# A two-layer hybrid trunk on one core: how the first weights of a new phase are prepared

## Chip, cores, metric

The kernel runs on one core of one Trainium2 chip. The metric is the device time of one execution in microseconds, as the median of several runs. The five engines are named as in the profile: PE (TensorE matmul, PEld its weight load), DVE (VectorE), ACT (ScalarE), POOL (GpSimd) and SP (SyncE, which issues the DMAs here).

## What is computed

256 tokens of width 2048 go through two layers, all in float32. Layer 0 mixes tokens with a Conformer convolution, layer 1 with differential attention; each is followed by a squared-ReLU MLP with 8192 hidden channels:

```python
for i in range(DEPTH):                                # DEPTH = 2
    mod = cond @ ada_w[i] + ada_b[i]                  # cond = silu(c)
    sh_m, sc_m, g_m, sh_f, sc_f, g_f = split(mod, 6)
    h = x * (1.0 + sc_m) + sh_m
    y = conformer_conv(h, ...) if i == 0 else diff_attention(h, ...)
    x = layer_norm(ALPHA * x + g_m * y, ln_mix_g[i], ln_mix_b[i])
    h = x * (1.0 + sc_f) + sh_f
    y = squared_relu_mlp(h, mlp_w1[i], ...)           # square(relu(h @ w1 + b1)) @ w2 + b2
    x = layer_norm(ALPHA * x + g_f * y, ln_ffn_g[i], ln_ffn_b[i])
```

## The kernel before

Every large product is made of three. A float32 operand is split into `hi`, a cast to the matmul's `fp32r` type on ACT, and `lo = x - hi` on DVE or POOL; PE then adds hi by hi (line 578), hi by the weights' lo (580) and lo by the weights' hi (581). Activations stand transposed in two buffers of 16 chunks of 128 channels each (`hm_hi` and `hm_lo` in the MLPs, `ha_hi` and `ha_lo` in the attention). Weights come in pieces of 1 MB, 128x2048, each handled as two **halves** of 128x1024: a half is one cast `wh_...`, one subtraction `wl_...` and, for two chunks and both token tiles, 12 matmuls of 128x512.

`run_jobs` walks a list of jobs, two halves each as a rule. `fetch(n)` prepares halves up to number n, four ahead of PE; their buffers rotate through four slots (`wsp`), so a half can be cast only when PE is through with the half four places earlier. ACT's order is left to the scheduler; PE's is as written, DVE's as written from the second convolution product on.

At three places the trunk goes from one weight matrix to one that needs the finished x of this one: convolution to first MLP (near 488 us of the trace), first MLP to attention (near 1232), attention to second MLP (near 1642). These are the **changes**. The last job before each (`tail`) has four halves; it does token tile 0 whole, then tile 1. So while PE works on tile 1, tile 0 is finished: `w2g`/`wo_g`/`pw_g` (line 727) multiplies by the gate, line 728 adds to `z`, then come statistics, `rs` (1/sqrt by a power on POOL, line 120), `nb` (653) and the normalising of four quarters of `z`, two on ACT (660), two on DVE (662). `feat_t` transposes the tile in four blocks on PE (`hm_t`, `ha_t`, 453), applies 1+scale and shift (`hm_h`, `ha_h`: blocks 0 and 2 on ACT, 458, blocks 1 and 3 on DVE, 461) and splits it (411 and 414; the lo of block 3 on POOL). The scale and shift columns come from `h_scalars` (740 to 743), which `prep` calls. The first job after a change (`lead`) has four halves as well and needs blocks 0 and 1 of a tile.

In `lead` jobs the subtractions of halves 1, 2 and 3 are POOL's (`POOL_LEAD`), in `tail` jobs those of halves 1 and 3. `base_x` multiplies `z` by the norm's gain (and in the attention adds its bias) on POOL, a quarter of the columns at a time (line 697, 699); `defer(first + step * q, ...)` sets after how many ticks. A tick is one half of an ordinary job.

## Time and profile before

| | |
|---|---|
| median of 3 runs | 2395.34 us (2389.94 to 2396.66) |
| the profiled execution | 2392.99 us, its span 2390.9 us |
| PE busy | 2279.8 us (95%) |
| PEld | 1816.8 us (76%) |
| DVE | 1763.9 us (74%) |
| ACT | 1095.2 us (46%) |
| POOL | 204.6 us (9%) |
| mean granted PE clock | 0.985 |

Times in the trace count from the start of the span; the 2.1 us by which the execution is longer lie around it. Busy shares are means over stages that differ, so PE at 95% leaves open where the other 5% lie.

### The profile page before, as it was taken

Reading aid. Unit: us, or ns where it says so; the run is one execution under the profiler, and the core shown is the slowest. Engines: PE = TensorE matmul, PEld = TensorE weight load, DVE = VectorE, ACT = ScalarE, POOL = GpSimd, SP = SyncE. Lnnn points to the kernel's source line nnn. Section 1 sums busy time; section 2 is a strip of 40 time slices with the busy share of each in tenths; the row PEclk is TensorE's granted clock in tenths of the full one; section 3 lists DMA queues with packets and bytes.
Section 4 is the critical chain, followed back from the end, with each engine's and each line's share of the span. In section 5 each row is a group of like instructions: output and inputs, shape, how many; then the busy total and the mean of one; then the engine's idle time right before and its main releaser. Section 6 shows DMA issues by size and latency. Waiting matters only on the chain.

```text
span 2390.9 us, 28653 instructions
## 1 busy us (share of the span) xinstructions
PE 2279.8 (95%) x11169; PEld 1816.8 (76%) x11169; DVE 1763.9 (74%) x2010; ACT 1095.2 (46%) x1498; POOL 204.6 (9%) x138
## 2 busy tenths in 40 slices
PE   5899998999999999999989999998999999999997
PEld 4576646778788888888867888876888888888885
DVE  5787787978787888878869776886875565555666
ACT  3333674255435445445444554544443443443442
POOL 0000001131200000000034001013111000000002
...
GB/s 346 331 321 305 134 250 384 347 187 331 319 323 289 313 316 280 318 315 284 301 182 240 228 181 235 235 315 134 297 257 204 183 194 194 181 189 194 193 219 98
DMA packets 270955, 606.47 MB, mean 254 GB/s; under 512 B 10974, under 2 KB 44388, under 8 KB 257508
## 3 DMA queue, kind: packets, MB, share of 16 engines
...
q14 instruction: 48, 0.39, 0.0%
...
## 4 chain that ended last, share of the span: by engine, by line
PE 79%; DVE 10%; DMA 4%; ACT 2%; issue 2%; SPq 1%; POOL 0%; DVEq 0%; ACTq 0%; POOLq 0%
PE w_ps L578 18%; PE w_ps L581 18%; PE w_ps L580 18%; DMA w_w<-in_mlp_w_dram 2%; DVE aacc L249 2%; PE pw_ps L503 2%; PE cv L784 2%; PE pw_ps L504 2%; PE pw_ps L505 2%; PE aps L290 1%; PE qkv_q_ps L581 1%; PE qkv_v_ps L581 1%; PE qkv_v_ps L578 1%; PE qkv_v_ps L580 1%; PE qkv_q_ps L580 1%
## 5 line engine op out<-in xcount | busy, mean ns | idle before, releaser
L543 DVE TENSOR_TENSOR wl_w<-w_w,wh_w 128x1024 fp32r<-128x1024 f32 x502 | 621.6, 1255 | 347.0 <-ACT wh_w L542 346.7
L542 ACT CAST wh_w<-w_w 128x1024 fp32r<-128x1024 f32 x512 | 539.2, 1056 | 736.6 <-PE w_ps L581 569.3
L578 PE MATMUL w_ps<-wh_w,hm_hi 128*128 128x512 f32 x1024 | 403.0, 394 | 4.5 <-ACT hm_hi L411 4.5
L580 PE MATMUL w_ps<-wl_w,hm_hi 128*128 128x512 f32 x1024 | 400.1, 391 | 2.4 <-DVE wl_w L543 2.4
L578 PE MATMUL w_ps<-wh_w,u_hi 128*128 128x512 f32 x1024 | 401.2, 392 | 0.0
L581 PE MATMUL w_ps<-wh_w,hm_lo 128*128 128x512 f32 x1024 | 400.1, 391 | 0.9 <-DVE hm_lo L414 0.9
L580 PE MATMUL w_ps<-wl_w,u_hi 128*128 128x512 f32 x1024 | 399.9, 391 | 0.0
L581 PE MATMUL w_ps<-wh_w,u_lo 128*128 128x512 f32 x1024 | 399.7, 390 | 0.0
L316 DVE SCALAR_TENSOR_TENSOR acc<-adaw,cond,acc 128x2048 f32<-128x2048 f32 (+1 forms) x105 | 243.9, 2323 | 0.1
L578 PEld LDWEIGHTS w_ps<-wh_w,hm_hi 128*128 128x128 f32 x1024 | 192.9, 188 | 48.5 <-ACT hm_hi L411 6.2
L580 PEld LDWEIGHTS w_ps<-wl_w,hm_hi 128*128 128x128 f32 x1024 | 192.9, 188 | 43.2 <-DVE wl_w L543 4.1
L581 PEld LDWEIGHTS w_ps<-wh_w,hm_lo 128*128 128x128 f32 x1024 | 192.7, 188 | 42.8 <-DVE hm_lo L414 2.7
L578 PEld LDWEIGHTS w_ps<-wh_w,u_hi 128*128 128x128 f32 x1024 | 192.9, 188 | 42.3 <-issue 1.7
L581 PEld LDWEIGHTS w_ps<-wh_w,u_lo 128*128 128x128 f32 x1024 | 193.0, 189 | 40.2
L580 PEld LDWEIGHTS w_ps<-wl_w,u_hi 128*128 128x128 f32 x1024 | 193.0, 188 | 40.0 <-DVE wl_w L543 0.2
L543 POOL TENSOR_TENSOR wl_w<-w_w,wh_w 128x1024 fp32r<-128x1024 f32 x10 | 24.0, 2405 | 1118.2 <-ACT wh_w L542 1118.2
L503 PE MATMUL pw_ps<-wh_pw,h_hi 128*128 128x512 f32 x256 | 107.0, 418 | 9.7 <-ACT wh_pw L491 4.1
L504 PE MATMUL pw_ps<-wl_pw,h_hi 128*128 128x512 f32 x256 | 102.7, 401 | 3.6 <-DVE wl_pw L492 3.6
L505 PE MATMUL pw_ps<-wh_pw,h_lo 128*128 128x512 f32 x256 | 102.3, 400 | 0.0
L492 DVE TENSOR_TENSOR wl_pw<-w_pw,wh_pw 128x1024 fp32r<-128x1024 f32 x64 | 77.8, 1222 | 26.2 <-ACT wh_pw L491 26.0
L491 ACT CAST wh_pw<-w_pw 128x1024 fp32r<-128x1024 f32 x64 | 66.0, 1052 | 48.6 <-PE pw_ps L505 40.8
L503 PEld LDWEIGHTS pw_ps<-wh_pw,h_hi 128*128 128x128 f32 x256 | 49.6, 194 | 39.0 <-issue 15.2
...
## 6 DMA issues: line engine op xcount, KB each, us to landing
w_w<-in_mlp_w_dram SPq DMA_DIRECT2D x256, 1024.0 KB, 5.6
...
```

The lines of the kernel that those rows point to most:

```text
L249: nc.vector.scalar_tensor_tensor(st["acc"], wv[:, kc % per, :], cond[:, kc:kc + 1], st["acc"], ALU.mult, ALU.add)
L316: nc.vector.scalar_tensor_tensor(st["acc"], w, cond[:, kc:kc + 1], st["acc"], ALU.mult, ALU.add)
L491: nc.scalar.copy(hq, rq)
L492: nc.vector.tensor_tensor(lq, rq, hq.bitcast(F32), op=ALU.subtract)
L503: nc.tensor.matmul(pss[t], lhsT=xh, rhs=wh, start=(kc == first), stop=False)
L504: nc.tensor.matmul(pss[t], lhsT=xh, rhs=wl, start=False, stop=False)
L505: nc.tensor.matmul(pss[t], lhsT=xl, rhs=wh, start=False, stop=(kc == last))
L542: nc.scalar.copy(hi, rq)
L543: eng.tensor_tensor(lo, rq, hi.bitcast(F32), op=ALU.subtract)
L578: nc.tensor.matmul(pss[tt], lhsT=xh, rhs=wh, start=(kc == 0 and job["bias"] is None), stop=False)
L580: nc.tensor.matmul(pss[tt], lhsT=xh, rhs=wl, start=False, stop=False)
L581: nc.tensor.matmul(pss[tt], lhsT=xl, rhs=wh, start=False, stop=(kc == nk - 1))
```

## The change

- The first halves of a `lead` job get buffers of their own: one half in the first MLP, two in the attention and the second MLP (`lead` is now that number). Half 0 lives in two buffers of the rotation `X`, half 1 in two new buffers of the pool `late`. They no longer wait for a slot, and `fetch` is called for them while PE is still at tile 0 of the `tail` job.
- `POOL_LEAD` is empty: all subtractions of `lead` halves are DVE's.
- In the attention and the second MLP `prep` (`h_scalars`) is called when the `tail` job begins.
- ACT runs in written order from the beginning of a `tail` job before a change to the end of the `lead` job, and only there.
- The fourth half's subtraction is written behind the blocks' steps (`low`), lo parts of the blocks are flushed earlier.
- `base_x` starts at 18 ticks in place of 6.

```diff
-POOL_LEAD = (1,2,3)
+POOL_LEAD = ()
...
+                    home = (None, "x", "late")[2 * i + q + 1] if lead and 2 * i + q < lead else None
+                    halves.append((f"{key}_{i}", srcs[i], q, pump, nc.gpsimd if pool else nc.vector, home))
...
+    def fetch(n, low=None):
...
-            hi = wsp.tile([P, 1024], F32R, tag="whi", name=f"wh_{name}_{q}")
-            lo = wsp.tile([P, 1024], F32R, tag="wlo", name=f"wl_{name}_{q}")
+            if home == "x":
+                hi = work.tile([P, 1024], F32R, tag="X", name=f"wh_{name}_{q}", bufs=3)
+                lo = work.tile([P, 1024], F32R, tag="X", name=f"wl_{name}_{q}", bufs=3)
+            elif home == "late":
+                hi = late["pool"].tile([P, 1024], F32R, tag="whi", name=f"wh_{name}_{q}")
+                lo = late["pool"].tile([P, 1024], F32R, tag="wlo", name=f"wl_{name}_{q}")
...
             nc.scalar.copy(hi, rq)
-            eng.tensor_tensor(lo, rq, hi.bitcast(F32), op=ALU.subtract)
+            if low is None:
+                eng.tensor_tensor(lo, rq, hi.bitcast(F32), op=ALU.subtract)
+            else:
+                low.append(lambda lo=lo, rq=rq, hi=hi, eng=eng: eng.tensor_tensor(
+                    lo, rq, hi.bitcast(F32), op=ALU.subtract))
...
+                nxt = jobs[n + 1] if n + 1 < len(jobs) else None
+                own, more = job["own"], nxt["own"] if nxt is not None else 0
+                if more:
+                    change = tc.manual_schedule(engines={mybir.EngineType.Activation})
+                    change.__enter__()
                 fetch(h + 4)
                 tail = []
+                if more and nxt["prep"] is not None and nxt["prep"][0]:
+                    nxt.pop("prep")[1]()
+                    nxt["prep"] = None
...
-                        if t == NT - 1:
-                            fetch(h + j + AHEAD)
+                        if t == NT - 1 and not more and not own:
+                            fetch(h + 4 + j)
+                        if t == NT - 1 and more and j >= 2:
+                            fetch(h + 4 + min(more + j - 1, 3))
                         steps = half(j, [t])
+                        if t == 0 and more and 1 <= j <= more:
+                            fetch(h + 4 + j)
+                        if t == NT - 1 and own:
+                            fetch(h + 4 + max(j + 1, own))
...
+                            low = []
                             if feat:
                                 feat.pop(0)()
+                                fetch(h + 4 + 4, low)
                             tail = steps[0]() or []
                             while tail or feat:
                                 if tail:
                                     tail.pop(0)()
+                                flush()
                                 if feat:
                                     feat.pop(0)()
+                                if low and not tail:
+                                    low.pop(0)()
...
+                if own:
+                    change.__exit__(None, None, None)
...
-            base_x(ln_g, None, f"basem{i}", 6, 4)
+            base_x(ln_g, None, f"basem{i}", 18, 4)
...
-                add_group(f"w1_{i}_{q}_{g}", lambda: cur["hT"], wtiles(mlp_w1[i], 0, KC, n0), pump=pump, lead=first,
+                add_group(f"w1_{i}_{q}_{g}", lambda: cur["hT"], wtiles(mlp_w1[i], 0, KC, n0), pump=pump, lead=(i + 1) * first,
...
-        base_x(ln_ffn_g[0], ln_ffn_b[0], "basea", 6, 5)
+        base_x(ln_ffn_g[0], ln_ffn_b[0], "basea", 18, 5)
```

How the instructions stand now is shown for the change into the attention; the change into the second MLP reads alike. PE's order is the same before and after throughout the program. VectorE first, at the end of the first MLP's tail job: `w2g_3_3_0` is the gating of tile 0, `wl_qkv_q_0_0` the first half of the attention's weights. Before:

```order
L727 TENSOR_TENSOR w2g_3_3_0_9481<-w_0_3_3_ps_9383,gbm_4883 128x512
L728 TENSOR_TENSOR z<-z,w2g_3_3_0_9481 128x512
L1276 BN_STATS mlp_st_3111<-z 128x6
L642 BN_AGGR lna_mv<-mlp_st_3111 128x2
L647 TENSOR_SCALAR lna_rs<-lna_mv 128x1
L543 TENSOR_TENSOR wl_qkv_q_0_0_9499<-w_qkv_q_0_9496,wh_qkv_q_0_0_9498 128x1024
L653 SCALAR_TENSOR_TENSOR lna_nb<-lna_mv,lna_rs 128x1
L662 TENSOR_SCALAR z<-z,lna_mv,lna_rs 128x512 x2
L740 TENSOR_SCALAR ha_s_9526<-mod_1_5845 128x16
L741 SCALAR_TENSOR_TENSOR ha_mul<-cols_ln,ha_s_9526 128x16
L742 TENSOR_TENSOR ha_add<-cols_ln,ha_s_9526 128x16
L743 TENSOR_TENSOR ha_add<-ha_add,mod_0_6880 128x16
```

After, where `ha_s` to `ha_add` are the scale and shift columns:

```order
L772 TENSOR_SCALAR ha_s_9464<-mod_1_5848 128x16
L773 SCALAR_TENSOR_TENSOR ha_mul<-cols_ln,ha_s_9464 128x16
L774 TENSOR_TENSOR ha_add<-cols_ln,ha_s_9464 128x16
L775 TENSOR_TENSOR ha_add<-ha_add,mod_0_6883 128x16
L552 TENSOR_TENSOR wl_qkv_q_0_0_9484<-w_qkv_q_0_9481,wh_qkv_q_0_0_9483 128x1024
L552 TENSOR_TENSOR wl_qkv_q_0_1_9494<-w_qkv_q_0_9481,wh_qkv_q_0_1_9493 128x1024
L759 TENSOR_TENSOR w2g_3_3_0_9503<-w_0_3_3_ps_9386,gbm_4886 128x512
L760 TENSOR_TENSOR z<-z,w2g_3_3_0_9503 128x512
L1308 BN_STATS mlp_st_3111<-z 128x6
L674 BN_AGGR lna_mv<-mlp_st_3111 128x2
L679 TENSOR_SCALAR lna_rs<-lna_mv 128x1
L685 SCALAR_TENSOR_TENSOR lna_nb<-lna_mv,lna_rs 128x1
```

The columns and two weight halves have moved ahead of tile 0's gating, where before they stood behind its normalising (the columns) or on POOL (half 1).

VectorE a little later, from tile 1's `rs` on, with the blocks 1, 0, 1 of tile 0. Before:

```order
L647 TENSOR_SCALAR lna_rs<-lna_mv 128x1
L461 TENSOR_SCALAR ha_h_9568<-ha_t_9567,ha_mul,ha_add 128x128 x4
L414 TENSOR_TENSOR ha_lo<-ha_h_9548,ha_hi 128x4x128
L653 SCALAR_TENSOR_TENSOR lna_nb<-lna_mv,lna_rs 128x1
L662 TENSOR_SCALAR z<-z,lna_mv,lna_rs 128x512 x2
L414 TENSOR_TENSOR ha_lo<-ha_h_9568,ha_hi 128x4x128
L461 TENSOR_SCALAR ha_h_9598<-ha_t_9597,ha_mul,ha_add 128x128 x4
L414 TENSOR_TENSOR ha_lo<-ha_h_9586,ha_hi 128x4x128
```

After, where `wl_qkv_q_1_1` is half 3 and the two `ha_h` rows in succession are block 3 of tile 0 and block 1 of tile 1:

```order
L679 TENSOR_SCALAR lna_rs<-lna_mv 128x1
L414 TENSOR_TENSOR ha_lo<-ha_h_9553,ha_hi 128x4x128
L461 TENSOR_SCALAR ha_h_9577<-ha_t_9576,ha_mul,ha_add 128x128 x4
L685 SCALAR_TENSOR_TENSOR lna_nb<-lna_mv,lna_rs 128x1
L694 TENSOR_SCALAR z<-z,lna_mv,lna_rs 128x512 x2
L414 TENSOR_TENSOR ha_lo<-ha_h_9577,ha_hi 128x4x128
L554 TENSOR_TENSOR wl_qkv_q_1_1_9564<-w_qkv_q_1_9530,wh_qkv_q_1_1_9563 128x1024
L414 TENSOR_TENSOR ha_lo<-ha_h_9595,ha_hi 128x4x128
L461 TENSOR_SCALAR ha_h_9608<-ha_t_9607,ha_mul,ha_add 128x128 x4
L461 TENSOR_SCALAR ha_h_9657<-ha_t_9656,ha_mul,ha_add 128x128 x4
```

The lo of block 0 now stands ahead of block 1's `ha_h`; half 3 has come in, and block 3 of tile 0 stands behind the lo of block 2.

ScalarE over the same stretch, from the first cast of the attention's weights on. Before:

```order
L542 CAST wh_qkv_q_0_0_9498<-w_qkv_q_0_9496 128x1024
L542 CAST wh_qkv_q_0_1_9514<-w_qkv_q_0_9496 128x1024
L542 CAST wh_qkv_q_1_0_9533<-w_qkv_q_1_9531 128x1024
L660 ACTIVATE z<-z,lna_nb,lna_rs 128x512 x2
L542 CAST wh_qkv_q_1_1_9612<-w_qkv_q_1_9531 128x1024
L458 ACTIVATE ha_h_9548<-ha_t_9547,ha_add,ha_mul 128x128 x4
L411 CAST ha_hi<-ha_h_9548 128x4x128
L411 CAST ha_hi<-ha_h_9568 128x4x128
L458 ACTIVATE ha_h_9586<-ha_t_9585,ha_add,ha_mul 128x128 x4
L411 CAST ha_hi<-ha_h_9586 128x4x128
L660 ACTIVATE z<-z,lna_nb,lna_rs 128x512 x2
L411 CAST ha_hi<-ha_h_9598 128x4x128
```

After:

```order
L550 CAST wh_qkv_q_0_0_9483<-w_qkv_q_0_9481 128x1024
L550 CAST wh_qkv_q_0_1_9493<-w_qkv_q_0_9481 128x1024
L692 ACTIVATE z<-z,lna_nb,lna_rs 128x512 x2
L550 CAST wh_qkv_q_1_0_9532<-w_qkv_q_1_9530 128x1024
L458 ACTIVATE ha_h_9553<-ha_t_9552,ha_add,ha_mul 128x128 x4
L411 CAST ha_hi<-ha_h_9553 128x4x128
L550 CAST wh_qkv_q_1_1_9563<-w_qkv_q_1_9530 128x1024
L411 CAST ha_hi<-ha_h_9577 128x4x128
L692 ACTIVATE z<-z,lna_nb,lna_rs 128x512 x2
L458 ACTIVATE ha_h_9595<-ha_t_9594,ha_add,ha_mul 128x128 x4
L411 CAST ha_hi<-ha_h_9595 128x4x128
L411 CAST ha_hi<-ha_h_9608 128x4x128
```

The casts of halves 2 and 3 have moved behind tile 0's normalising and behind block 0's split.

## Rows read from the trace of the kernel before

**Rows 1.** Timeline, TensorE, attention change: start us, us, instruction, count [idle before <-releaser].

```profile
1231.83 0.39 PE L581 MATMUL w_ps<-wh_w,u_lo 128*128 128x512 f32 x1
1234.27 1.97 PE L453 MATMUL ha_t<-ident,z 128*128 128x128 f32 x16 [2.06 <-ACT z L660]
1242.68 0.80 PE L578 MATMUL qkv_q_ps<-wh_qkv_q,ha_hi 128*128 128x512 f32 x1 [6.44 <-ACT ha_hi L411]
...
1245.37 0.79 PE L581 MATMUL qkv_q_ps<-wh_qkv_q,ha_lo 128*128 128x512 f32 x1 [1.47 <-DVE ha_lo L414]
1245.96 0.63 PE L578 MATMUL qkv_q_ps<-wh_qkv_q,ha_hi 128*128 128x512 f32 x1
1246.39 0.63 PE L580 MATMUL qkv_q_ps<-wl_qkv_q,ha_hi 128*128 128x512 f32 x1
...
1255.28 0.50 PE L578 MATMUL qkv_q_ps<-wh_qkv_q,ha_hi 128*128 128x512 f32 x1 [0.94 <-ACT ha_hi L411]
...
1262.38 0.50 PE L580 MATMUL qkv_q_ps<-wl_qkv_q,ha_hi 128*128 128x512 f32 x1 [0.52 <-DVE wl_qkv_q L543]
```

**Rows 2.** Timeline, TensorE, attention to second MLP.

```profile
1642.07 0.39 PE L581 MATMUL wo_ps<-wh_wo,attno_lo 128*128 128x512 f32 x1
...
1672.38 0.50 PE L580 MATMUL w_ps<-wl_w,hm_hi 128*128 128x512 f32 x1 [1.34 <-DVE wl_w L543]
```

**Rows 3.** Timeline, ScalarE, attention change.

```profile
1228.17 1.06 ACT L542 CAST wh_qkv_q<-w_qkv_q 128x1024 fp32r<-128x1024 f32 x1 [5.74 <-PE w_ps L581]
...
1240.46 1.51 ACT L458 ACTIVATE ha_h<-ha_t,ha_add,ha_mul 128x128 f32<-128x128 f32 x4 [4.60 <-DVE ha_add L743]
1242.01 0.62 ACT L411 CAST ha_hi<-ha_h 128x512 fp32r<-128x512 f32 x1
...
1247.48 1.52 ACT L660 ACTIVATE z<-z,lna_nb,lna_rs 128x512 f32<-128x512 f32 x2
```

**Rows 4.** Timeline, VectorE, attention change.

```profile
1229.37 1.23 DVE L543 TENSOR_TENSOR wl_qkv_q<-w_qkv_q,wh_qkv_q 128x1024 fp32r<-128x1024 f32 x1
1231.04 2.33 DVE L653 SCALAR_TENSOR_TENSOR lna_nb<-lna_mv,lna_rs 128x1 f32<-128x1 f32 x1 [0.44 <-POOL lna_rs L120]
...
1238.17 2.20 DVE L743 TENSOR_TENSOR ha_add<-ha_add,mod 128x16 f32<-128x16 f32 x1
1240.29 0.68 DVE L727 TENSOR_TENSOR w2g<-w_ps,gbm 128x512 f32<-128x512 f32 x1
...
1245.31 0.99 DVE L662 TENSOR_SCALAR z<-z,lna_mv,lna_rs 128x512 f32<-128x512 f32 x2
...
1248.29 0.69 DVE L414 TENSOR_TENSOR ha_lo<-ha_h,ha_hi 128x512 fp32r<-128x512 f32 x1
1253.58 1.37 DVE L461 TENSOR_SCALAR ha_h<-ha_t,ha_mul,ha_add 128x128 f32<-128x128 f32 x4 [4.61 <-PE ha_t L453]
```

**Rows 5.** Timeline, GpSimd, attention change.

```profile
1222.51 2.39 POOL L543 TENSOR_TENSOR wl_w<-w_w,wh_w 128x1024 fp32r<-128x1024 f32 x1 [3.05 <-ACT wh_w L542]
...
1237.97 2.36 POOL L543 TENSOR_TENSOR wl_qkv_q<-w_qkv_q,wh_qkv_q 128x1024 fp32r<-128x1024 f32 x1
1242.98 0.55 POOL L120 TENSOR_TENSOR lna_rs<-lna_rs,neg_half 128x1 f32<-128x1 f32 x1 [2.65 <-DVE lna_rs L647]
```

**Rows 6.** Windows: busy us and count of PE, PEld, DVE, ACT, POOL; PEclk; DMA.

```profile
1235.00:1236.00 1.00, 1.00 (x12) 1.00 (x10) 1.00 (x1) 0.86 (x1) 1.00 (x1) 1.00 0.79 276
1249.00:1250.00 1.00, 1.00 (x5) 0.82 (x4) 0.00 (x0) 0.51 (x2) 0.41 (x1) 0.74 0.00 0
```

**Rows 7.** Timeline, TensorE, convolution to first MLP, and later in that MLP.

```profile
492.22 1.11 PE L453 MATMUL hm_t<-ident,z 128*128 128x128 f32 x4 [2.59 <-ACT hm_h L458]
...
505.64 0.50 PE L578 MATMUL w_ps<-wh_w,hm_hi 128*128 128x512 f32 x1
...
606.71 0.55 PE L333 MATMUL adpt<-ident,adrow 96*128 96x96 f32 x4 [2.32 <-ACT adrow L327]
```

**Rows 8.** Windows, as above, in the second MLP's first quarter.

```profile
1700.00:1710.00 10.00, 10.00 (x50) 8.29 (x49) 10.00 (x7) 4.24 (x5) 4.96 (x2) 1.00 1.01 364
```

More of the change, by code (lines that the diff above doesn't have):

```diff
@@ L523, in add_group @@
             first = blk[0] == 0
-            jobs.append(dict(key=key, pair=pair, n=2 * len(blk), kc0=blk[0] * per, nk=per * len(srcs),
+            jobs.append(dict(key=key, pair=pair, n=2 * len(blk), own=int(lead) if first else 0, kc0=blk[0] * per, nk=per * len(srcs),
                              start=start if first else None, pre_t=pre_t if first else None, pre_done=False, prep=prep if first else None, on_t=on_t, bias=bias if first else None,
@@ L530, in add_group @@
                             or 2 * i + q in on_pool)
-                    halves.append((f"{key}_{i}", srcs[i], q, pump, nc.gpsimd if pool else nc.vector))
-    def fetch(n):
+                    home = (None, "x", "late")[2 * i + q + 1] if lead and 2 * i + q < lead else None
+                    halves.append((f"{key}_{i}", srcs[i], q, pump, nc.gpsimd if pool else nc.vector, home))
+    def fetch(n, low=None):
         while len(split) < min(n, len(halves)):
-            name, src, q, pump, eng = halves[len(split)]
+            name, src, q, pump, eng, home = halves[len(split)]
             if q == 0:
@@ L539, in fetch @@
             rq = raws["raw"][:, q * 1024:(q + 1) * 1024]
-            hi = wsp.tile([P, 1024], F32R, tag="whi", name=f"wh_{name}_{q}")
-            lo = wsp.tile([P, 1024], F32R, tag="wlo", name=f"wl_{name}_{q}")
-            nc.scalar.copy(hi, rq)
-            eng.tensor_tensor(lo, rq, hi.bitcast(F32), op=ALU.subtract)
+            if home == "x":
[5 more added lines that the diff above has]
+            else:
+                hi = wsp.tile([P, 1024], F32R, tag="whi", name=f"wh_{name}_{q}")
+                lo = wsp.tile([P, 1024], F32R, tag="wlo", name=f"wl_{name}_{q}")
+            nc.scalar.copy(hi, rq)
+            if low is None:
+                eng.tensor_tensor(lo, rq, hi.bitcast(F32), op=ALU.subtract)
+            else:
+                low.append(lambda lo=lo, rq=rq, hi=hi, eng=eng: eng.tensor_tensor(
+                    lo, rq, hi.bitcast(F32), op=ALU.subtract))
             per = src.shape[1] // 2
@@ L600, in run_jobs @@
                             job["between"](GF_USE[2 * t + 1])
-                        if t == NT - 1:
-                            fetch(h + j + AHEAD)
+                        if t == NT - 1 and not more and not own:
+                            fetch(h + 4 + j)
+                        if t == NT - 1 and more and j >= 2:
+                            fetch(h + 4 + min(more + j - 1, 3))
                         steps = half(j, [t])
+                        if t == 0 and more and 1 <= j <= more:
+                            fetch(h + 4 + j)
+                        if t == NT - 1 and own:
+                            fetch(h + 4 + max(j + 1, own))
                         if steps and t == 0:
                             tail = steps[0]() or []
-                            nxt = jobs[n + 1] if n + 1 < len(jobs) else None
                             if nxt is not None and nxt["prep"] is not None:
-                                tail.append(nxt["prep"])
+                                tail.append(nxt["prep"][1])
                         elif steps:
@@ L1267, in mlp @@
                 first = q == 0 and g == 0
-                add_group(f"w1_{i}_{q}_{g}", lambda: cur["hT"], wtiles(mlp_w1[i], 0, KC, n0), pump=pump, lead=first,
+                add_group(f"w1_{i}_{q}_{g}", lambda: cur["hT"], wtiles(mlp_w1[i], 0, KC, n0), pump=pump, lead=(i + 1) * first,
                           start=(lambda q=q: begin_q(q)) if g == 0 else None,
-                          pre_t=pre_t if first else None, on_t=on_t1, prep=prep if first else None,
+                          pre_t=pre_t if first else None, on_t=on_t1, prep=(i == 1, prep) if first else None,
                           between=ada_between if first and i == 0 else None)
@@ L1512, in trunk @@
         pair = lambda: sc1["hT"]
-        add_group(f"qkv_q{g}", pair, wtiles(attn_qkv_w[0], 0, KC, g * NG), pump=pump_slow, lead=(g == 0),
-                  start=begin_attn if g == 0 else None, prep=prep_attn if g == 0 else None, pre_t=pre_attn if g == 0 else None,
+        add_group(f"qkv_q{g}", pair, wtiles(attn_qkv_w[0], 0, KC, g * NG), pump=pump_slow, lead=2 * (g == 0),
+                  start=begin_attn if g == 0 else None, prep=(True, prep_attn) if g == 0 else None, pre_t=pre_attn if g == 0 else None,
                   on_t=rope_evac("q", g, kv))
```

## The prediction

> **What bounds the kernel now.** I read the waits of TensorE first, then its timeline round the three changes, then the timelines of the engines it waited for. Inside a phase TensorE runs without a gap; what can be saved without making its work smaller lies where it stands still, and the changes are three such places. The attention's shows it best. The tail's last matmul is issued at 1231.83; at about 0.23 us a matmul the next could go at 1232.06, which I call E. There follow 2 us of waiting for the normalised z, 16 transposes (1.97 us), 6.44 us until `ha_hi`, two matmuls, 1.47 us until `ha_lo` [rows 1]. Tile 1's first product starts at 1255.28, and the second matmul of half 4, from which the stream is dense again, at 1262.38, that is E + 30.3. The same point of the second MLP is 1672.38 against E = 1642.30, so 30.1 [rows 1, 2]. The work in between is two times 24 matmuls (10.9 us) and 32 transposes (3.9 us); nearly half of the 30 us is waiting or slow clock.
>
> What ends the long wait is read from ScalarE: its `ha_h` started at 1240.46 after 4.60 us without work, released by `ha_add` [rows 3]. On VectorE `ha_add`, on 128x16 elements, took 2.20 us, from 1238.17 to 1240.37; GpSimd's `wl_qkv_q` ran from 1237.97 to 1240.33. `lna_nb`, on one column, took 2.33 us likewise [rows 4, 5]. So these small instructions stood until GpSimd's subtraction was done: the subtractions that POOL_LEAD gives to GpSimd hold VectorE on the path.
>
> The slow clock is the second part: matmuls follow each other in 0.43 us at 1245.96 and 1246.39, and only in the slice 1249 to 1250 does the granted clock go from 0.5 (1.2 GHz) to 1.0 (2.4 GHz), its mean being 0.74 [rows 1, 6]. TensorE had idled for 6.44 us ahead of these matmuls and was dense for some 4 us before the rise.
>
> **The change, attention.** Durations: cast of a half 1.06, subtraction 1.23 on VectorE, two quarters normalised 1.52 on ScalarE and 1.0 on VectorE, a block's `ha_h` 1.51 and 1.37, its hi 0.62, its lo 0.69, GpSimd's power 0.55 alone [rows 3 to 5]. Tile 1's gating, statistics and `rs`, five instructions, begin at 1240.29, and the power on the result at 1242.98: 2.6 us and a hand-over of 0.1 [rows 4, 5].
>
> Up to E: halves 0 and 1 wait for no slot any more and are cast beside tile 0 of the tail. VectorE takes their subtractions when GpSimd's last one of the tail ends (1222.51 + 2.39 = 1224.9), so they are done at 1227.4; then gating and `rs` of tile 0 (2.6), power (0.55) and `nb` with 0.1 to 0.2 us of hand-over each: 1230.8. ScalarE's quarters are normalised at 1232.3, E + 0.25, where before `lna_nb` alone ended at 1233.37. The columns cost nothing on the way: they are done before the first cast. Cover gone, they would cost four small instructions, under 1 us.
>
> From E, each step behind the one it needs:
> - ScalarE: half 2's cast to E+1.3, `ha_h` of block 0 to E+2.85, its hi to E+3.45. First matmul at **E+3.5** (before: E+10.6).
> - VectorE: half 2's lo to E+2.5, tile 1's gating and `rs` to E+5.1, lo of block 0 to E+5.8. Third matmul at E+5.85 (before: 1245.37, E+13.3). This wait of near 2 us is what is late next: the lo stands behind tile 1's gating.
> - VectorE: `ha_h` of block 1 to E+7.1, tile 1's quarters to E+8.2, lo of block 1 to E+8.9, half 3's lo to E+10.1. TensorE, at 0.23 us, takes each just after it comes and ends tile 0 at E+11.3.
> - ScalarE: tile 1's quarters to E+9.25, block 2 to E+11.35. VectorE: lo of block 2 to E+12.1, and only then `ha_h` of block 3 (to E+13.4) and block 1 of tile 1. Block 3's hi ends at E+14.05, block 0 of tile 1 at E+15.55, its hi at E+16.15. Tile 1's first matmul at **E+16.2** (before: E+23.2).
> - 24 matmuls and a short wait for a lo: E+22. Half 4's lo, cast only behind the blocks, ends at E+22.15. Dense from **E+22.2** in place of E+30.3: **8.1 us**.
>
> Three subtractions of 1.23 us have come to VectorE per change (3.7 us) and are in these sums; GpSimd's three of 2.4 us have gone with what they held up.
>
> The clock makes the size uncertain. Before, the fall came in the 6.44 us; now the pieces are 1.3, 1.9 and 2.3 us. Nearest rows: after the 2.06 us ahead of the transposes the clock was still 1.00, from 1235 to 1236; after 6.44 us it was low [rows 1, 6]. If it falls once, up to 15 matmuls (the 6.8 us from 1242.68 to 1249.5 that it stayed low) cost 0.2 us more each, 3.1 us. Bounds 8.1 and 5.0; the pieces are nearer to 2.06 but come in succession, so I take a little under half the price: **6.7 us**.
>
> **The second MLP** has the same order and the same rows: 7.9 to 4.8, **6.6 us**.
>
> **The first MLP.** Here products of the modulation (`aps`) stand between, the columns stay late, and one half has its own buffers. Before, the fourth block's transposes waited 2.59 us, to 492.22, for ScalarE to free a PSUM bank [rows 7]. Now GpSimd no longer slows the quarters and `hm_add`; by the same steps ScalarE frees the bank at 490.2, 2 us sooner, and tile 1's first matmul, 505.64 before [rows 7], comes at about 503.3, again behind `hm_h` of block 3 on VectorE. **2.3 us**; bounds 0 (an interposed product's data is late anyway) and 3.
>
> **Off the changes.** ScalarE's order near 606 us differs too, where a transpose of `adrow` waited 2.32 us behind a cast [rows 7]; `adrow` now stands ahead of that cast: gain 0 to 2.3. The base passes move from the gaps into dense stretches, three to four quarters in each phase, with their DMAs of 256 KB. The row nearest to that: from 1700 to 1710 GpSimd ran two passes in 4.96 us, VectorE was busy 10.00 of 10.00, and TensorE too [rows 8]: cost 0 there. Bound: 2.5 us a phase if one pair of passes comes through to TensorE each time. I set gain and cost against each other: 0, with +2.3 and -7.5 as ends.
>
> The Trainium skill, page "SBUF — State Buffer", section "SBUF: two separate sides", says that VectorE with two SBUF inputs and GpSimd take a shared port pair by turns, each for a whole instruction, the other fully blocked. `ha_add` agrees. By it each moved pass stops VectorE for its whole length, which would turn the sum of 15.6 us into the loss of the second rival if VectorE had no slack; by the row from 1700 the sum stays.
>
> **Sum:** 6.7 + 6.6 + 2.3 = 15.6 us off the profiled execution's 2392.99, so 2377.4. That execution was 2.35 us below the median; off the median it gives **2379.7**, say 2379.5.
>
> **Rivals.**
> - *The clock eats it.* It falls in both gaps of each change, as the successive waits would let it, and tile 1, dense at 2.4 GHz before, is done at 1.2. Then the attention and the second MLP give some 4 us each and the first MLP 1: 2386. For it: two waits of 2 us within 15. Against: the transposes between them ran at full clock before. Chance 0.16.
> - *The base passes go through to TensorE* (the other side). 32 multiplications and additions in dense stretches, 2.48 us each where they share with VectorE [rows 8], are 79 us. It decides when over 15.6 of these, a fifth, reach TensorE; at 0.3% (7.2 us) more, 29%. A third gives +10.7: 2406. Against it stands TensorE's 10.00 of 10.00 beside them. Slower 0.04; a part of it that eats the gain to within 0.3% (near 2390), 0.06.
> - *The early halves don't help.* VectorE's three subtractions, or a piece of weights that lands late, keep block 0's lo where it was, and only the 2 us waits for the columns go: some 2 to 3 us a change, 2387. For it: those three lie ahead of block 0's lo or of tile 1's. Against it: `nb` and `ha_add` alone stood 4.3 us behind GpSimd [rows 4]. Chance 0.08, part of it within 0.3%.
>
> **Numbers.** Forecast 0.66; clock 0.16; no help 0.08; base passes 0.10. The forecast's own range is 2374 (full 8.1, 7.9, 2.3, with 2.3 from `adrow`) to 2384. The range of 2373 to 2388 takes in the clock case and the no-help case and leaves out the base passes and a gain beyond all upper bounds. 0.3% is about what a measurement here can tell from no change. Faster by more: forecast, clock and most of no help, 0.87; within 0.09; slower 0.04.
>
> **What would show it.** Right: no subtraction of the first halves on GpSimd; `ha_add` and `nb` at 0.2 us; first matmul near E+3.5, tile 1's near E+16, dense near E+22 to E+24. TensorE's wait for `ha_hi` falls from 6.44 us to under 2.5, and a new wait shows at the lo of block 0 and at tile 1's first block. Wrong: a granted clock of 0.5 behind E+16; TensorE waiting for `wl_w` from 550 to 590 or from 1690 to 1730 where base passes now run; the tail's tile 0 gating late because a first half's cast is.

## The result, and the profile after

The changed kernel takes 2376.67 us (median of 6 runs, 2374.66 to 2382.21), the kernel before on the same chip 2392.64 us (2388.29 to 2397.39): ratio 0.9946, 95% interval 0.9933 to 0.9960, 16.0 us less. The forecast was 2379.5 us, 15.6 us less than the 2395.34 that it started from. The profiled execution of the changed kernel is the longest of its six (2382.21 us, span 2380.4 us), so its span is only 10.5 us under that of before; where those 10.5 us come from is read below, and the missing ones are the first experiment's subject.

The waits of TensorE, the rows that answer to the long waits of before (total us, times, longest us):

```profile
PE qkv_q_ps L590 <- ACT ha_hi L411: 3.2, 2, 2.1
...
PE w_ps L590 <- ACT hm_hi L411: 3.2, 2, 2.1
...
PE qkv_q_ps L593 <- DVE ha_lo L414: 2.2, 2, 1.6
PE gbm_p L703 <- DVE mod L336: 2.1, 1, 2.1
```

`ha_hi` was waited for 6.44 us at the longest [rows 1], now 2.1, and the waits for `z` (2.06 us at the attention, [rows 1], and 2.05 at the second MLP) are gone. New in size are the waits for the lo pieces. The timeline of TensorE at the attention change says where each stands (start us, us, instruction, count, idle before and its releaser). E is 1235.01 here, since the transposes follow the tail's last matmul without a gap:

```profile
1235.01 1.91 PE L453 MATMUL ha_t<-ident,z 128*128 128x128 f32 x16
1238.04 0.50 PE L590 MATMUL qkv_q_ps<-wh_qkv_q,ha_hi 128*128 128x512 f32 x1 [1.12 <-ACT ha_hi L411]
...
1240.39 0.50 PE L593 MATMUL qkv_q_ps<-wh_qkv_q,ha_lo 128*128 128x512 f32 x1 [1.61 <-DVE ha_lo L414]
...
1245.67 1.47 PE L453 MATMUL ha_t<-ident,z 128*128 128x128 f32 x12
1247.79 0.66 PE L453 MATMUL ha_t<-ident,z 128*128 128x128 f32 x4 [0.65 <-DVE ha_h L461]
1250.50 0.50 PE L590 MATMUL qkv_q_ps<-wh_qkv_q,ha_hi 128*128 128x512 f32 x1 [2.05 <-ACT ha_hi L411]
...
1251.79 0.51 PE L593 MATMUL qkv_q_ps<-wh_qkv_q,ha_lo 128*128 128x512 f32 x1 [0.55 <-DVE ha_lo L414]
...
1252.52 0.63 PE L592 MATMUL qkv_q_ps<-wl_qkv_q,ha_hi 128*128 128x512 f32 x1
...
1255.08 0.63 PE L592 MATMUL qkv_q_ps<-wl_qkv_q,ha_hi 128*128 128x512 f32 x1
...
1258.73 0.39 PE L592 MATMUL qkv_q_ps<-wl_qkv_q,ha_hi 128*128 128x512 f32 x1
```

First product at E + 3.0 (before E + 10.6), third at E + 5.4 (E + 13.3), tile 1's first at E + 15.5 (E + 23.2), dense from 1258.73, E + 23.7 (E + 30.3). From 1252.52 to 1255.08 the products follow each other in 0.43 us: the clock is at its lower level. VectorE and ScalarE in the same stretch:

```profile
1224.33 0.17 DVE L775 TENSOR_TENSOR ha_add<-ha_add,mod 128x16 f32<-128x16 f32 x1
...
1233.28 0.16 DVE L685 SCALAR_TENSOR_TENSOR lna_nb<-lna_mv,lna_rs 128x1 f32<-128x1 f32 x1 [0.66 <-POOL lna_rs L120]
...
1239.65 0.68 DVE L414 TENSOR_TENSOR ha_lo<-ha_h,ha_hi 128x512 fp32r<-128x512 f32 x1
...
1245.77 0.69 DVE L414 TENSOR_TENSOR ha_lo<-ha_h,ha_hi 128x512 fp32r<-128x512 f32 x1 [1.43 <-ACT ha_hi L411]
1246.38 1.36 DVE L461 TENSOR_SCALAR ha_h<-ha_t,ha_mul,ha_add 128x128 f32<-128x128 f32 x4
```

```profile
1247.77 0.62 ACT L411 CAST ha_hi<-ha_h 128x512 fp32r<-128x512 f32 x1 [2.04 <-DVE ha_h L461]
1248.30 1.50 ACT L458 ACTIVATE ha_h<-ha_t,ha_add,ha_mul 128x128 f32<-128x128 f32 x4
1249.83 0.62 ACT L411 CAST ha_hi<-ha_h 128x512 fp32r<-128x512 f32 x1
```

`ha_add` takes 0.17 us and `lna_nb` 0.16 (2.20 and 2.33 before, [rows 4]). The third product waits for the lo at 1239.65, which VectorE makes behind tile 1's statistics. Tile 1's first product waits for the hi at 1249.83, this for block 0 of tile 1 at 1248.30, which stands on ScalarE behind block 3's hi (1247.77); that one waited 2.04 us for VectorE's `ha_h` of block 3 (1246.38), which stands behind the lo of block 2 (1245.77).

TensorE at the second MLP (E = 1637.67) and at the first:

```profile
1637.67 1.91 PE L453 MATMUL hm_t<-ident,z 128*128 128x128 f32 x16
...
1653.16 0.50 PE L590 MATMUL w_ps<-wh_w,hm_hi 128*128 128x512 f32 x1 [2.05 <-ACT hm_hi L411]
...
1661.42 0.39 PE L592 MATMUL w_ps<-wl_w,hm_hi 128*128 128x512 f32 x1
```

```profile
490.94 0.66 PE L453 MATMUL hm_t<-ident,z 128*128 128x128 f32 x4 [1.14 <-ACT hm_h L458]
...
503.73 0.50 PE L590 MATMUL w_ps<-wh_w,hm_hi 128*128 128x512 f32 x1
...
505.60 0.63 PE L590 MATMUL w_ps<-wh_w,hm_hi 128*128 128x512 f32 x1
...
508.12 0.39 PE L590 MATMUL w_ps<-wh_w,hm_hi 128*128 128x512 f32 x1
```

The second MLP is dense from E + 23.75 (before E + 30.1). In the first MLP the bank comes free at 490.94 (before 492.22, [rows 7]; the forecast was 490.2) and tile 1 starts at 503.73 (505.64), but from 505.60 to 508.12 the clock is low, and the product at 508.12 began at 508.09 before: all of the lead is gone.

From such timelines the lengths of the stages, by the first matmul of each, in us:

| stage of TensorE's work | before | changed | changed, second execution |
|---|---|---|---|
| start to the convolution's last matmul | 488.16 | 488.32 | 485.81 |
| from there to `apt` near 515, the first MLP's change | 27.28 | 27.16 | 24.88 |
| to `gbm_p` near 612 | 96.80 | 99.79 | 97.60 |
| to the attention's E | 619.82 | 619.74 | 619.34 |
| to the second MLP's E | 410.24 | 402.66 | 402.07 |
| to the last matmul | 732.06 | 726.31 | 726.17 |

### The profile page after: what moved, and what is told of

The parts are those of the page before. It is cut to its first block, busy times and chain, and to the rows that moved or that the text cites. A ratio compares the mean times of both kernels' runs of the same rounds, so it can differ in the third digit from the quotient of the medians.

```text
span 2380.4 us, 28638 instructions
## 1 busy us (share of the span) xinstructions
PE 2277.5 (96%) x11169; PEld 1815.9 (76%) x11169; DVE 1755.9 (74%) x2019; ACT 1093.3 (46%) x1498; POOL 180.3 (8%) x129
## 4 chain that ended last, share of the span: by engine, by line
PE 79%; DVE 11%; DMA 4%; ACT 3%; issue 2%; SPq 1%; POOL 0%; DVEq 0%; ACTq 0%
PE w_ps L593 18%; PE w_ps L590 18%; PE w_ps L592 18%; DVE aacc L249 2%; PE pw_ps L503 2%; PE cv L816 2%; PE pw_ps L504 2%; PE pw_ps L505 2%; PE qkv_v_ps L593 1%; PE qkv_v_ps L590 1%; PE qkv_v_ps L592 1%; PE qkv_q_ps L593 1%; PE qkv_q_ps L590 1%; PE qkv_q_ps L592 1%; PE qkv_k_ps L593 1%
## 5 line engine op out<-in xcount | busy, mean ns | idle before, releaser
L552 DVE TENSOR_TENSOR wl_w<-w_w,wh_w 128x1024 fp32r<-128x1024 f32 x506 | 632.1, 1265 | 361.2 <-ACT wh_w L550 358.1
L492 DVE TENSOR_TENSOR wl_pw<-w_pw,wh_pw 128x1024 fp32r<-128x1024 f32 x64 | 77.8, 1221 | 27.0 <-ACT wh_pw L491 24.1
L552 POOL TENSOR_TENSOR wl_w<-w_w,wh_w 128x1024 fp32r<-128x1024 f32 x4 | 9.6, 2396 | 1115.1 <-ACT wh_w L550 1115.1
L503 PEld LDWEIGHTS pw_ps<-wh_pw,h_hi 128*128 128x128 f32 x256 | 49.5, 193 | 39.4 <-issue 15.8
```

Source lines behind the costliest of these rows:

```text
L492: nc.vector.tensor_tensor(lq, rq, hq.bitcast(F32), op=ALU.subtract)
L503: nc.tensor.matmul(pss[t], lhsT=xh, rhs=wh, start=(kc == first), stop=False)
L552: eng.tensor_tensor(lo, rq, hi.bitcast(F32), op=ALU.subtract)
```

## The experiments

Twelve runs, of the changed kernel itself and ten others; all edits are to the changed kernel but where it is said. Medians are in us, ratios to the kernel before on the same chip with their 95% interval. The columns behind them are worked out from TensorE's timeline of each profile: first and third product, tile 1's first, dense stream, in us behind E (a matmul missing from a trace shifts the last by 0.2).

| kernel | median | ratio, interval | attention: first, third, tile 1, dense | second MLP: dense |
|---|---|---|---|---|
| before | | 1 | 10.6, 13.3, 23.2, 30.3 | 30.1 |
| changed | 2376.67 | 0.9946, 0.9933 to 0.9960 | 3.0, 5.4, 15.5, 23.7 | 23.8 |
| changed, again | 2376.16 | 0.9945, 0.9928 to 0.9962 | 3.0, 5.4, 15.5, 22.2 | 23.7 |
| no own buffers | 2387.91 | 1.0000, 0.9988 to 1.0013 | 7.8, 10.1, 20.2, 26.9 | 26.9 |
| before, subtractions on VectorE | 2383.93 | 0.9983, 0.9974 to 0.9992 | 5.4, 9.1, 19.8, 26.9 | 26.4 |
| subtractions on GpSimd | 2382.41 | 0.9963, 0.9950 to 0.9976 | 3.4, 4.4, 15.5, 23.8 | 23.7 |
| the same, again | 2380.77 | 0.9953, 0.9940 to 0.9966 | 3.4, 4.4, 15.5, 23.8 | 23.7 |
| base passes early | 2376.51 | 0.9942, 0.9929 to 0.9955 | 3.0, 5.8, 15.9, 24.1 | 24.7 |
| columns late | 2380.63 | 0.9957, 0.9945 to 0.9970 | 5.1, 6.0, 16.1, 22.8 | 24.3 |
| ScalarE by the scheduler | 2372.02 | 0.9923, 0.9908 to 0.9937 | 4.0, 4.9, 14.1, 20.2 | 24.3 |
| block 3 first | 2371.07 | 0.9922, 0.9907 to 0.9937 | 3.0, 5.4, 13.8, 20.0 | 20.8 |
| lo of block 0 first | 2377.83 | 0.9951, 0.9938 to 0.9964 | 3.0, 4.2, 15.4, 23.6 | 23.6 |
| both first | 2371.84 | 0.9919, 0.9907 to 0.9931 | 3.0, 4.2, 13.6, 19.9 | 20.0 |
| block 3 first, half 2 on GpSimd | 2369.03 | 0.9910, 0.9896 to 0.9924 | 3.0, 4.5, 12.8, 19.1 | 19.1 |

**The changed kernel again.** No edit.

> The changed kernel once more, nothing edited. In its first profile the second MLP and the attention gained 6.3 and 6.6 us against the kernel before, but between 508 and 640 us it lost 3 us, and that execution lies 5.5 us above the median of its six. Theory A (those 3 us are one execution's transfers in a stage where the DMA engines are the limit): the changes again reach the dense stream at E + 23.7 within 0.3 us, and the stretch from 508 to 640 comes out at another value, by 2 us or more. Theory B (the moved base passes cost it every time): the stretch is again 3 us longer than in the kernel before, within 1 us.

Theory A for that stretch: to `gbm_p` it is 97.60 us, 2.2 less than in the first profile and 0.8 more than before. Transfers are shown for a part of the difference. In the first profile a cast on ScalarE waited 3.56 us for weights to land, and the copy `us`, which stands behind it, came so late that TensorE waited 1.93 us for it, to 552.04; in the second the same cast waited 0.79 us and TensorE did not wait there. First profile:

```profile
550.46 1.04 ACT L550 CAST wh_w<-w_w 128x1024 fp32r<-128x1024 f32 x1 [3.56 <-DMA w_w<-in_mlp_w_dram]
551.41 0.58 ACT L1274 COPY us<-w_ps 128x512 f32<-128x512 f32 x1
```

The first MLP's change, with nothing edited, gives 2.4 us where it gave 0.1. The attention came out 1.5 us better than A said, and its timeline tells why:

```profile
1227.64 1.91 PE L453 MATMUL ha_t<-ident,z 128*128 128x128 f32 x16
...
1233.59 0.63 PE L592 MATMUL qkv_q_ps<-wl_qkv_q,ha_hi 128*128 128x512 f32 x1
...
1236.15 0.63 PE L592 MATMUL qkv_q_ps<-wl_qkv_q,ha_hi 128*128 128x512 f32 x1
...
1239.76 1.91 PE L453 MATMUL ha_t<-ident,z 128*128 128x128 f32 x16
1243.11 0.51 PE L590 MATMUL qkv_q_ps<-wh_qkv_q,ha_hi 128*128 128x512 f32 x1 [1.44 <-ACT ha_hi L411]
```

The clock fell here too, and for as many products, but in tile 0, from 1233.59 to 1236.57. Tile 0 ends later for it, and the wait ahead of tile 1 is shorter by nearly as much; tile 1's first product is at E + 15.5 as before and its row runs at full clock. A window of each execution, first this one, then the first (busy us and count of PE, PEld, DVE, ACT, POOL; then PEclk):

```profile
1233.50:1237.00 3.50, 3.50 (x11) 2.69 (x9) 3.44 (x8) 2.74 (x6) 0.00 (x0) 0.51 0.00 0
```

```profile
1252.20:1255.50 3.30, 3.30 (x9) 2.53 (x8) 2.37 (x6) 3.23 (x8) 0.78 (x1) 0.50 0.00 0
```

So one fall of the clock costs 1.5 us or nothing, by the tile that it meets.

**No own buffers.** The first halves take the common slots; the order of instructions is the same on all five queues.

```diff
-                    home = (None, "x", "late")[2 * i + q + 1] if lead and 2 * i + q < lead else None
+                    home = None
```

> The changed kernel with the first halves in the common slots; every engine's order of instructions stays the same. Theory A (the early casts need the own buffers): the tail's four halves hold the four slots, the first comes free only when tile 1 of the tail has passed it, near E - 4.1; the two subtractions, which stand ahead of the tail's tile 0 gating on VectorE, end near E - 0.5 instead of E - 5, the gating follows, and the first matmul comes near E + 7.5 instead of E + 3.0. Some 4.5 us lost at the attention and at the second MLP, 1 to 3 at the first MLP: 10 to 13 us slower than the changed kernel, most of the gain. Theory B (GpSimd's subtractions were the whole matter): under 3 us slower in all.

Theory A, in size too: it is 11.7 us slower than the changed kernel on the same chip by the medians, and the ratio to the kernel before is 1.000. TensorE and the two engines ahead of it:

```profile
1236.19 3.68 PE L453 MATMUL ha_t<-ident,z 128*128 128x128 f32 x16 [3.95 <-ACT z L692]
```

```profile
1228.20 1.05 ACT L550 CAST wh_qkv_q<-w_qkv_q 128x1024 fp32r<-128x1024 f32 x1 [5.75 <-PE w_ps L593]
1229.62 1.05 ACT L550 CAST wh_qkv_q<-w_qkv_q 128x1024 fp32r<-128x1024 f32 x1 [0.36 <-PE w_ps L593]
```

```profile
1229.29 1.22 DVE L552 TENSOR_TENSOR wl_qkv_q<-w_qkv_q,wh_qkv_q 128x1024 fp32r<-128x1024 f32 x1 [7.71 <-ACT wh_qkv_q L550]
1230.70 1.23 DVE L552 TENSOR_TENSOR wl_qkv_q<-w_qkv_q,wh_qkv_q 128x1024 fp32r<-128x1024 f32 x1 [0.19 <-ACT wh_qkv_q L550]
1231.85 0.68 DVE L759 TENSOR_TENSOR w2g<-w_ps,gbm 128x512 f32<-128x512 f32 x1
```

The first cast waits 5.75 us for TensorE to leave a slot; VectorE stands 7.71 us, then subtracts twice and begins the tail's tile 0 gating at 1231.85, 0.2 us ahead of E (1232.09); in the changed kernel it begins at 1230.00, 5.0 us ahead. The transposes wait 3.95 us for `z`, and at 3.68 us in place of 1.91 they run at the lower clock (0.50). In this profile the attention and the second MLP are still dense 3.4 and 3.2 us sooner than in the kernel before, while tile 1 of the first MLP starts 2.0 us later (19.5 us behind the convolution's last matmul, 17.5 before). This execution is the shortest of its ten; over all ten nothing is left of the gain.

**The subtractions on VectorE alone.** The kernel before with one constant changed.

```diff
-POOL_LEAD = (1,2,3)
+POOL_LEAD = ()
```

> The kernel before with one constant changed: the subtractions of halves 1 to 3 are on VectorE, nothing else. Theory A (part of the gain is GpSimd's hold on VectorE): ha_add and lna_nb fall to 0.2 us, but three subtractions of 1.23 us stand in VectorE's row at the change; the wait for ha_hi falls from 6.4 to 3 or 4 us, and the whole is 4 to 8 us faster than the kernel before. Theory B (without halves in hand early nothing is won, since VectorE takes over what GpSimd gives up): within 2 us of the kernel before.

Theory A at its lower end: about 4 us of the 16, and the interval leaves out 1.

```profile
1236.53 0.50 PE L578 MATMUL qkv_q_ps<-wh_qkv_q,ha_hi 128*128 128x512 f32 x1 [2.77 <-ACT ha_hi L411]
...
1240.19 0.79 PE L581 MATMUL qkv_q_ps<-wh_qkv_q,ha_lo 128*128 128x512 f32 x1 [2.92 <-DVE ha_lo L414]
```

The wait for `ha_hi` is 2.77 us instead of 6.44. `lna_nb` falls to 0.16 us, `ha_add` only to 1.19, since a base pass of GpSimd (1232.93 to 1234.20) stands beside it. The halves are still late: the first cast waits 5.75 us for a slot, and VectorE subtracts halves 0 to 2 between 1228.45 and 1235.36, ahead of tile 1's gating.

**The subtractions back on GpSimd,** in the changed kernel, twice (the edit above the other way round).

> The changed kernel with the subtractions of halves 1 to 3 back on GpSimd; own buffers, early fetch and order stay. Theory A (a GpSimd subtraction stops VectorE's instructions on two SBUF operands till it ends): the subtractions of halves 2 and 3, 2.4 us each, fall on tile 1's gating and the first lo pieces; small instructions of 0.2 to 0.7 us show as 2 us and more, the third matmul and tile 1's first come 2 to 3 us later, and the whole is 5 to 8 us slower than the changed kernel. Theory B (early halves alone are what helps, and GpSimd takes work off VectorE): 0 to 4 us faster than the changed kernel.

> The kernel with the subtractions of halves 1 to 3 back on GpSimd, once more. Its first profile reached tile 1 at the attention and the second MLP as early as the changed kernel (E + 15.5) and lost 1.5 us at the first MLP, but the median of its executions lay 6 us above the changed kernel's. Theory A (with own buffers it hardly matters where the subtractions run: VectorE loses about as much to the hold as it gains in free time): ratio to the kernel before within 0.0015 of 0.9945, and the changes again at E + 15.5. Theory B (GpSimd's subtractions cost some 4 to 6 us even with own buffers): ratio again near 0.9963, with a place in the trace where 3 us or more are lost.

Of the first text theory B fails (no gain), and theory A fails at the attention and the second MLP: tile 1 starts at E + 15.5 with or without them, though by the medians the whole is 6 us slower than the changed kernel on the same chip. Of the second text theory A holds (0.9953 and E + 15.5). The hold itself is there, on both engines:

```profile
1220.32 2.58 DVE L552 TENSOR_TENSOR wl_qkv_q<-w_qkv_q,wh_qkv_q 128x1024 fp32r<-128x1024 f32 x1 [1.86 <-ACT wh_qkv_q L550]
...
1224.45 1.27 DVE L760 TENSOR_TENSOR z<-z,w2g 128x512 f32<-128x512 f32 x1
...
1229.89 0.69 DVE L760 TENSOR_TENSOR z<-z,w2g 128x512 f32<-128x512 f32 x1
...
1234.55 1.59 DVE L685 SCALAR_TENSOR_TENSOR lna_nb<-lna_mv,lna_rs 128x1 f32<-128x1 f32 x1
```

```profile
1221.78 3.38 POOL L552 TENSOR_TENSOR wl_qkv_q<-w_qkv_q,wh_qkv_q 128x1024 fp32r<-128x1024 f32 x1
...
1233.73 2.40 POOL L554 TENSOR_TENSOR wl_qkv_q<-w_qkv_q,wh_qkv_q 128x1024 fp32r<-128x1024 f32 x1
```

`lna_nb`, one column, takes 1.59 us and ends at 1236.14, with GpSimd's subtraction (1233.73 + 2.40 = 1236.13). Adding into `z` takes 1.27 us where GpSimd is at work till 1225.16, and 0.69 alone. GpSimd's subtraction from 1221.78 takes 3.38 us instead of 2.40: VectorE's subtraction of half 0 runs beside its first 1.1 us, to 1222.90. But VectorE is rid of 3.7 us of subtractions, and the two nearly cancel. At the first MLP tile 1 starts at +16.0 and +15.8 us behind the convolution's last matmul, against 15.4 and 14.5 in the changed kernel. The ratios, 0.9963 and 0.9953, lie 0.001 to 0.002 above the changed kernel's with overlapping intervals: a cost of 2 to 4 us is likely, but its place beyond the first MLP is not found.

**The base passes at their old place.**

```diff
-            base_x(ln_g, None, f"basem{i}", 18, 4)
+            base_x(ln_g, None, f"basem{i}", 6, 4)
...
-        base_x(ln_ffn_g[0], ln_ffn_b[0], "basea", 18, 5)
+        base_x(ln_ffn_g[0], ln_ffn_b[0], "basea", 6, 5)
```

> The changed kernel with the base passes back at their old place, 6 ticks behind the start of a phase instead of 18. Theory A (moving them later cost nothing to the dense stretch, and is worth something at the changes): GpSimd's passes of 1.2 to 2.4 us each fall between the two powers of the change and on VectorE's small instructions; dense stream later than E + 23.7 by 2 us or more at the attention and the second MLP, the whole 3 to 8 us slower. Theory B (the passes in the dense stretch cost 3 us in the first MLP): that stretch is 3 us shorter than in the changed kernel, and the whole within 2 us of it or faster.

Neither in full. The changes lose 0.4 and 0.9 us. The stretch to `gbm_p` is 95.33 us here; over the three profiles with early passes (before, before with the subtractions on VectorE, this) its median is 96.1, over the eleven with late ones 97.5, two of these running to 99.8 and 101.2: some 1.4 us, with one execution of each kernel. TensorE's waits for `wl_w` in that stretch sum to 0.9 us here, 1.1 in the kernel before, 2.0 and 3.3 in the two profiles of the changed kernel. From the dense point of the second MLP to the end, the three take 701.9 to 702.0 us (before: 732.06 - 30.08), the eleven 702.4 to 702.9: half a microsecond. In the attention, from its dense point to the second MLP's E, it is 379.4 to 379.9 us against 378.8 to 382.7, which shows nothing. It shows as one wait for a `wl_w` behind GpSimd's passes; these are TensorE's waits from 1664 to 1760 in the changed kernel, and with early passes there are none:

```profile
PE w_ps L592 <- DVE wl_w L552: 0.8, 1, 0.8
```

In the total the move shows no gain and no cost (0.9942 against 0.9946 and 0.9945).

**The columns late.**

```diff
-                          pre_t=pre_t if first else None, on_t=on_t1, prep=(i == 1, prep) if first else None,
+                          pre_t=pre_t if first else None, on_t=on_t1, prep=(False, prep) if first else None,
...
-... prep=(True, prep_attn) if g == 0 else None, ...
+... prep=(False, prep_attn) if g == 0 else None, ...
```

> The changed kernel with the columns of h's scale and shift made at their old place at the attention and the second MLP, behind the tail's tile 0 normalising. Theory A (VectorE's row decides): the four small instructions stand behind the subtraction of half 2, so ScalarE's block 0 waits till E + 2.9, the first matmul comes near E + 5.0 instead of E + 3.0, the third near E + 6.1, but tile 1's first matmul only 0.6 us later, E + 16.1: 1 to 2 us slower in all, within what a comparison shows. Theory B (the columns early are a main part of the gain): 4 us or more slower.

By the trace theory A within 0.2 us: first 5.1, third 6.0, tile 1 16.1. The time is 4 us above the changed kernel's by the medians and 3 by the ratios, with overlapping intervals, which does not settle it between the two.

**ScalarE's order left to the scheduler.** The region of written order and its end are left out.

```diff
-                    change = tc.manual_schedule(engines={mybir.EngineType.Activation})
-                    change.__enter__()
...
-                    change.__exit__(None, None, None)
```

> The changed kernel without the written order on ScalarE: the scheduler puts half 2's cast ahead of tile 0's normalising, half 3's ahead of block 0, half 4's ahead of block 2, and block 2's scaling ahead of block 1's hi. Theory A (the written order is part of the gain): the casts stand in the way of the blocks, tile 1's first matmul comes 1 us or more later than E + 15.5, 2 to 5 us slower than the changed kernel. Theory B (the order by itself is worth nothing, since the slots are free by then): block 2 is scaled as soon as its buffer is free, near E + 5.3, its hi comes 1.2 us sooner, and with it VectorE's block 3; tile 1's first matmul near E + 14.4, 0 to 5 us faster.

Theory B: 4 to 5 us faster than the changed kernel by the medians, the interval overlapping those of its two measurements by 0.0004 and 0.0009. The casts come early and block 2 is scaled at E + 4.8:

```profile
1228.06 1.98 ACT L550 CAST wh_qkv_q<-w_qkv_q 128x1024 fp32r<-128x1024 f32 x2
...
1232.89 1.50 ACT L458 ACTIVATE ha_h<-ha_t,ha_add,ha_mul 128x128 f32<-128x128 f32 x4 [0.82 <-DVE ha_lo L414]
```

At the attention tile 1 starts at E + 14.1. At the second MLP it starts at E + 14.5, but a wait of 2.1 us for a lo follows and the clock, which had already fallen in tile 0, falls again in tile 1, dense at E + 24.3. The written order shows as no part of the gain.

**Block 3 first.** VectorE scales block 3 of tile 0 ahead of the lo of block 2.

```diff
-                                flush()
+                                if len(feat) != 2: flush()
```

> The changed kernel, with VectorE scaling block 3 of tile 0 ahead of the lo of block 2 (the flush ahead of block 3 left out). Theory A (tile 1's first block waits on ScalarE behind block 3's hi, which waits for VectorE): block 3 is scaled while ScalarE still makes block 2's hi, tile 1's first matmul comes near E + 13.5 instead of E + 15.5, and where the clock no longer falls another 1.6 us: 2 to 3.5 us at each of the attention and the second MLP, 0 to 3 at the first MLP, in all 4 to 9 us faster than the changed kernel. Theory B (something else gates tile 1, such as its normalising or the bank of the transposes): within 1.5 us.

Theory A: tile 1 at E + 13.8 at the attention, at E + 14.7 at the second MLP, where the clock fell in tile 0; 5 us less by the medians (the intervals overlap as little as in the kernel above); at the attention the waits round tile 1's start sum to 1.4 us in place of 3.3:

```profile
1227.84 1.91 PE L453 MATMUL ha_t<-ident,z 128*128 128x128 f32 x16
...
1241.59 0.50 PE L590 MATMUL qkv_q_ps<-wh_qkv_q,ha_hi 128*128 128x512 f32 x1 [1.19 <-ACT ha_hi L411]
...
1242.49 0.50 PE L593 MATMUL qkv_q_ps<-wh_qkv_q,ha_lo 128*128 128x512 f32 x1 [0.16 <-DVE ha_lo L414]
```

**The lo of block 0 first.** It comes right behind tile 1's gating, ahead of its statistics.

```diff
-                    add_gated(ps, gate["gb"], t, n, f"w2g_{i}_{q}_{n}_{t}")
+                    add_gated(ps, gate["gb"], t, n, f"w2g_{i}_{q}_{n}_{t}"); flush() if q == n == 3 and t == NT - 1 else None
...
-                add_gated(ps, gate["gb"], t, q, f"{name}_g{q}{t}")
+                add_gated(ps, gate["gb"], t, q, f"{name}_g{q}{t}"); flush() if q == 3 and t == NT - 1 else None
```

> The changed kernel, with VectorE making the lo of block 0 right behind tile 1's gating and ahead of its statistics. Theory A (the third matmul waits only because the lo stands behind tile 1's statistics): third matmul at E + 4.2 instead of E + 5.4, tile 0's 24 matmuls end 1.2 us sooner; but tile 1's first matmul hangs on the blocks behind it and not on TensorE, so it comes at E + 15.5 or up to 0.3 later, the wait ahead of it 1.2 us longer; the whole within 1.5 us of the changed kernel. Theory B (each microsecond of TensorE's wait in tile 0 counts): 2.4 to 3.6 us faster.

Theory A: the third product comes at E + 4.2, tile 1 at E + 15.4, no gain. The wait of 1.6 us for the lo was hidden behind the later one.

**Both first.**

> Both reorderings together. Theory A: block 3 early sets tile 1 free, so that the lo's 1.2 us now count: tile 1's first matmul near E + 13, dense stream near E + 20 at the attention and the second MLP where the clock holds; 5 to 11 us faster than the changed kernel. Theory B (VectorE's row is full and only moves the wait): no more than the better of the two edits by itself, within 1 us.

In the trace theory A for the dense stream (E + 19.9 and 20.0, no fall of the clock in tile 1), but tile 1 comes at E + 13.6 and 13.7, at the attention only 0.1 us sooner than with block 3 first alone: the 1.2 us of the lo do not count there. In the time theory B: 2371.84 against 2371.07.

**Block 3 first, and half 2's subtraction on GpSimd** (`POOL_LEAD = (2,)`).

> The changed kernel with VectorE scaling block 3 ahead of the lo of block 2, and half 2's subtraction alone on GpSimd. Theory A (with block 3 early, VectorE's row behind E is the limit, and 1.2 us taken from it count): tile 1's first matmul near E + 12.6 instead of E + 13.8, dense stream near E + 19, 0 to 3 us faster than with block 3 early alone, 5 to 8 faster than the changed kernel. Theory B (the hold takes back what VectorE gains): the two powers and the lo of block 0 end with GpSimd's subtraction, E + 13.8 or later, no gain over block 3 early alone.

Theory A: tile 1 at E + 12.8, dense at E + 19.1 at both changes, 2369.03 us. Its interval (0.9896 to 0.9924) lies under the changed kernel's; that it beats block 3 first alone is not shown. At the first MLP it loses: tile 1 starts 16.6 us behind the convolution's last matmul, with block 3 first alone 14.4. The clock (PEclk) stays at its full level through both changes:

```profile
1230.00:1262.00 32.00, 28.84 (x139) 22.86 (x138) 24.87 (x42) 22.52 (x37) 6.37 (x4) 1.00 0.40 139
1629.00:1660.00 31.00, 27.85 (x135) 22.04 (x134) 23.22 (x39) 22.44 (x39) 6.37 (x4) 1.00 0.40 134
```

## Why the prediction was right

**Attention, 6.7 us predicted (8.1 to 5.0).** 6.6 in the first profile, 8.15 in the second: the clock fell in tile 1 in one and not in the other. The steps held within 0.8 us: first product E + 3.5 (3.0), third 5.85 (5.4), tile 1 16.2 (15.5), dense 22.2 without a fall (22.2). The chain named for tile 1, ScalarE's block 0 behind block 3's hi behind VectorE, is shown by moving block 3.

**Second MLP, 6.6 us.** 6.3 and 6.4, with a fall each time.

**First MLP, 2.3 us (0 to 3).** 0.1 and 2.4, by the clock again. The three together gave 13.0 us in the first profile and 16.9 in the second; the forecast of 15.6 lies between.

**The clock.** Before, 12 products began at the lower level at the attention (1242.68 to 1249.37), not the 15 that the price of 3.1 us was made of; now 8, in one fall. Taking a little under half of 3.1 us was near the 1.5 that one fall costs, but by luck, not for the reason given: the fall need not be split over two gaps, it is free where the tile that it meets ends ahead of what tile 1 waits for. Two signs that were named as wrong showed all the same, too small to undo the gain: in the first profile the clock was low from E + 17.5 at the attention, and from 550 to 590 TensorE waited for `wl_w` 1.2 and 3.0 us in the two profiles (1.1 before).

**Off the changes, 0 us.** `adrow`'s wait of 2.32 us [rows 7] is gone, but `gbm_p` waits 2.1 us for VectorE in that stretch, and the stretch is no shorter. The moved passes cost half a microsecond at the second MLP and likely some 1.4 at the first, of the 7.5 that were the bound. VectorE has some room for them: in the second MLP it is busy 88% without passes (1697 to 1737, base passes early) and 99% with them (1693 to 1736, changed kernel). The hold that the Trainium skill states (page "SBUF — State Buffer", section "SBUF: two separate sides") shows in the 1.59 us of `lna_nb`; the trace agrees with the rule, and the sum was right to go by the row from 1700 [rows 8].

**What the argument weighed wrongly.** It put GpSimd's hold first. Moving the subtractions off GpSimd is by itself worth 4 of the 16 us in the kernel before, and with own buffers perhaps 2 to 4; taking the own buffers away loses 11.7 us, and the ratio is back at 1.000. It took ScalarE's written order as given and costed nothing for it; the scheduler's order is some 4 us better, by intervals that barely overlap. And the columns, "under 1 us" without cover, cost 2.0 us at the first product, though 0.6 at tile 1, which counts. The later subtraction of the fourth half and the earlier flush were not taken out by themselves, so what they are worth is not shown.

**The rivals.** "The early halves don't help" fails by the kernel without own buffers. "The base passes go through to TensorE" fails: some 2 us come through in place of the 15.6 that it needed. "The clock eats it" is real in mechanism (all of the first MLP's gain in one execution), but in the changed kernel the clock falls once a change and not twice.
